# Shorter TensorE bursts, later uses of transposed data and a fourth weight buffer in a two-layer hybrid decoder trunk

## The chip, the cores and the metric

The kernel runs on one core of one Trainium2 chip. The metric is device time in microseconds (us) of one launch; lower is better. A core has a matrix engine (TensorE, in the profile PE for products and PEld for weight loads), a vector engine (VectorE, DVE), an activation engine (ScalarE, ACT), GpSimd (POOL) and SyncE (SP), which here only issues DMA transfers. Each engine works through its own queue in order and waits on semaphores for the others. SBUF is the on-chip memory, PSUM the memory into which TensorE writes its products.

## The reference

Two layers over 256 tokens of width 2048, batch 1, all in float32:

```python
for l in range(DEPTH):                                   # DEPTH = 2
    hn = rms_norm(h, norm_w[l])
    proj = hn @ w_in[l]                                  # 2048 x 8208
    dn_qkv, dn_z, dn_b, dn_a, hg_q, hg_f, hg_i, hg_z = split(proj)
    y_a = deltanet_branch(dn_qkv, dn_z, dn_b, dn_a, ...) # 8 heads of 128: conv, SiLU, L2 norm,
                                                         # gated delta rule with a triangular solve
    y_b = hgrn2_branch(hg_q, hg_f, hg_i, hg_z, ...)      # 8 heads of 128: gated linear recurrence
    h = h + concat(y_a, y_b) @ w_out[l]                  # 2048 x 2048
    gate = sigmoid(h @ w_ple_gate[l])                    # 2048 x 2048
    h = h + (p[l] @ w_ple_up[l]) * gate                  # 256 x 2048
return rms_norm(h, final_norm_w)
```

## The kernel before

**Weight steps.** All weights are streamed once from HBM. `make_plan` cuts them into 392 steps, most of them 128 x 1024 numbers (two blocks of 128 rows by 512 columns, 512 KB). For each step SP loads a tile `raw` (`load`), ACT rounds it into `whi`, DVE forms the rest `wlo = raw - whi` (`prep`), and TensorE multiplies (`products`, through line 378): hi by hi, hi by lo and lo by hi, for both halves of the tokens, 12 matmuls of 128 x 512 in a usual step. `ahead(n)` keeps loads four steps and `whi`/`wlo` two steps ahead of TensorE. There are three buffers `raw` (`WRAW = 3`) and three of `whi` and `wlo`.

**Chunks.** A layer is an input stage ("in", 17 chunks), an output stage ("out", 4) and a gate stage ("gate", 4, with "up"). A chunk is up to 512 columns that accumulate in two PSUM banks, one for each half of the tokens, out of three (`pd`). At its end ACT copies the banks out: `evict` (tiles `...et`), `gate_z` (`...zs`) and `hi` (`...iv`). The first step of the next chunk writes its second bank, which is the first bank of the chunk that has just ended, so TensorE waits there for ACT. The name of a tile tells its owner: `dn12kqet` is DeltaNet, layer 1, head pair 2, keys and queries, evicted.

**Mixers beside the weight steps.** Eight mixers per layer (DeltaNet `DN` and HGRN2 `HG`, each for head pairs g = 0 to 3) and one triangular inverse (`Inverse`, tiles `di`) are Python generators. `tick()` runs after each weight step and advances each of them whose delay, counted in steps, is over. The delays are in the tables `DELAY` and `DELAY_AT` (key: kind, pair or layer, step). TensorE's order is kept exactly as it is written; on the other engines a scheduler sets the order from it. The small float32 products of the mixers stand between two weight steps. One such product is two matmul records and two weight loads in the profile, so 64 products are 256 records. The places in question are `pa1` (64 products in one `tick`, HG), `pa16` (32 products, HG) and the stages `pp16`, `px16` (64 each), `pp32`, `px32`, `pp64`, `px64` (32 each) of `Inverse.run`.

**Transposes by DMA.** Several results must be turned by 128 x 128. Some go through TensorE (`turned`, `turn`: four matmuls against the identity into a PSUM bank). Others go by DMA: `apart` lets ACT split the numbers into 16-bit planes and write them to HBM from ACT's queue, `across` reads them back transposed from SP's queue (line 568), and a later step of the generator uses the result. By DMA go k and q of all four DeltaNet pairs (`kq`), f and q of all four HGRN2 pairs (`fq`), v of pairs 0 to 2 (`v` and, after the convolution, `pv`), five of eight results y (`yp`), and three quarters of h between the stages (`g0`, `n1`, `g1`).

Of the kernel before, what the change touches and what calls it, by code (L numbers as in the profile page):

```python
# [8 lines left out]
F32 = mybir.dt.float32  # L9
# [24 lines left out]
def chunk_cols(chunk):  # L34
# [5 lines left out]
DELAY = {  # L40
# [4 lines left out]
}  # L45

DELAY_AT = {
# [14 lines left out]
}  # L62


V_DMA = 0, 1, 2
Y_DMA = 0, 1, 2, 4, 5
# [110 lines left out]
def trunk(ctx: ExitStack, tc: tile.TileContext, head, xT, x, pT, W, par, fw, cst, msk, eye, out):  # L177
# [3 lines left out]
    hp = pool("hres", 1)  # L181
    ap_ = pool("acts", 13)
    wr = pool("wraw", 3)
    ws = pool("wsplit", 3)
# [6 lines left out]
    V, S, G = nc.vector, nc.scalar, nc.gpsimd  # L191
    WRAW = 3

# [182 lines left out]
    class PEOrder:  # L376
        def matmul(self, *a, **k):
            return tc.keep_in_program_order(nc.tensor.matmul(*a, **k))  # L378

# [3 lines left out]
    PE = PEOrder()  # L383
    live = []

    def spawn(gen):
        live.append([gen, 0])
        advance(live[-1])
# [24 lines left out]
    LOOK, LOAD = 2, 4  # L413
    state = dict(next=0, loaded=0, prepped=0, squared=0)

# [58 lines left out]
    def run_step(psums, act):  # L474

        n = state["next"]
        s = steps[n]
        ahead(n)
        for parts in (range(3),) if s["first"] or s["last"] else ((0, 1), (2,)):
            for m in range(2):  # L480
                products(n, m, psums, act, parts=parts)
        del ready[n]
        state["next"] = n + 1
        if s["what"] != "up":
            tick()
        return s
# [64 lines left out]
    def apart(src, name, into=None):  # L551

        n, c = src.shape[1:]
        for t in range(n):
            yield 1
            if not t:
                flat = (tmp if n * c == 512 else et_tile)(name + "pl") if into is None else into
                flat = u16(flat).rearrange("p (n w c) -> p n w c", n=n, w=2)
            S.copy(flat[:, t], u16(src[:, t]).rearrange("p (c w) -> p w c", w=2))
        d = dr.tile([256 * n * c], U16, tag=f"tr{n * c}", name=name + "d", bufs=4)  # L560
        nc.scalar.dma_start(out=d.rearrange("(n p x) -> p n x", n=n, p=128), in_=flat.rearrange("p n w c -> p n (w c)"))
        return d, c, n * c
# [131 lines left out]
    class Inverse:  # L694
# [24 lines left out]
        def run(self):  # L719
# [38 lines left out]
            pp = bank("pp16")  # L758
            for i in range(NT):
                for b in blocks:  # L760
                    PE.matmul(pp[b:b + 32, 16 * i:16 * i + 16], Bt[b:b + 32, i, b:b + 32], Tn[b:b + 32, i, 0:16],
                              start=True, stop=True)
# [4 lines left out]
            px = bank("px16")  # L767
            for i in range(NT):
                for b in blocks:
                    PE.matmul(px[b:b + 32, 16 * i:16 * i + 16], Pp[b:b + 32, 32 * i:32 * i + 32],  # L770
                              Tt[b:b + 32, i, b + 16:b + 32], start=True, stop=True)
# [5 lines left out]
            for b in (0, 64):  # L777
                V.transpose(Tn[b:b + 32], Tt[b:b + 32, :, b:b + 32])
            yield self.wait("t32")
            pp = bank("pp32")  # L780
            for i in range(NT):
# [4 lines left out]
            for b in (0, 64):  # L786
                S.copy(Pp[b + 32:b + 64], pp[b + 32:b + 64])
            yield self.wait("p32")
            px = bank("px32")
            for i in range(NT):  # L790
# [9 lines left out]
            for T, sl in zip(Tn, parts):  # L800
# [3 lines left out]
                V.transpose(T[32:64, :, 0:32], Tt[0:32, sl, 32:64])  # L804
            yield self.wait("t64")
            pp = [bank(f"pp64{j}") for j in range(len(parts))]
            for i in range(NT):
# [5 lines left out]
            for P_, p in zip(Pp, pp):  # L813
                S.copy(P_[64:128], p[64:128])
            yield self.wait("p64")
            px = [bank(f"px64{j}") for j in range(len(parts))]
            for i in range(NT):
# [8 lines left out]
    class DN:  # L826
# [145 lines left out]
        def dv(self, ps, c0):  # L972
            n, kq, g = self.n, self.kq, self.g
            et, e = evict(ps, c0, 256, self.row.rt, n + "v")
            if g in V_DMA:
                x = yield from apart(et, n + "v", e[:, 512:1024])
                yield self.wait("ve")
                t = across(x, n + "v")
                yield self.wait("vc")
            else:  # L980
                yield self.wait("vp")
                t = turned(et, 0, n + "pvc")
# [3 lines left out]
            V.tensor_tensor(ac, ac, sg, ALU.mult)  # L986
            if g in V_DMA:
                x = yield from apart(ac.unsqueeze(1), n + "pv")
# [63 lines left out]
    class HG:  # L1052
# [19 lines left out]
        def hfhq(self, ps, c0):  # L1072
            x = yield from apart(evict(ps, c0, 512, self.row.rt, self.n + "fq")[0], self.n + "fq")
            yield self.wait("e")
            t = across(x, self.n + "fq")
            yield self.wait("c")
            spawn(self.f_side(t[:, 0:512]))
            spawn(self.q_side(t[:, 512:1024]))

# [17 lines left out]
        def q_side(self, qr):  # L1097
# [76 lines left out]
            xs += factors((8,))  # L1174
            yield self.wait("a")

            A = hA
            Ad = mix("hAd", 128, 1, n + "Ad").rearrange("p (i c) -> p i c", i=4)
            pa = bank("1")
            for i in range(4):  # L1180
                for b in range(0, 128, 32):
                    PE.matmul(pa[b:b + 32, 48 * i:48 * i + 48], k4[:, i, b:b + 32], q8[:, 4 * i + b // 32, :],
                              start=True, stop=True)
            products(UNITS[1:4], xs, pa, 192)
            w1 = pa[:, :192].rearrange("p (i c) -> p i c", c=48)
# [7 lines left out]
            xs += factors((64,))  # L1193
            yield self.wait("u16")
            pb = bank("16")
            products(UNITS[4:], xs, pb, 384)
# [342 lines left out]
```

## Time and profile before

| What | us |
|---|---|
| median of 3 runs (1246.39 to 1248.14) | 1247.51 |
| the profiled execution, its own time | 1244.3 |
| its span, from first to last instruction | 1242.6 |
| TensorE busy, share of the span | 1203.8 (97%) |
| VectorE busy | 877.7 (71%) |
| ScalarE busy | 829.5 (67%) |
| DMA, mean rate | 206 GB/s |

The span is the profiled execution from its first to its last instruction; the 1.7 us beside it lie outside. "Busy" on TensorE counts a matmul from its start to its modelled end, and matmuls overlap: 97% busy does not mean that no time is lost, because slow and stretched matmuls count as well. A view of waits names for each idle stretch the instruction that came next and what released it; "issue" there means that the profile shows nothing that the engine waited for. The granted clock (PEclk) is the share of its full clock that TensorE was given.

### The profile page before, as it was taken

What the parts mean: (1) busy time and instruction counts of PE and PEld (TensorE: products, weight loads), DVE (VectorE), ACT (ScalarE), POOL (GpSimd) and SP (SyncE); (2) the same over time, 40 slices, a digit from 0 to 9 for tenths busy, and PEclk for the clock granted to TensorE, in tenths of its full rate; (3) what the DMA queues carried; (4) which work ended last, traced back from release to release, by engine and by line L of the source; (5) the groups of instructions that cost most, each with busy time, mean ns of one, the idle gap of its engine ahead of it and who ended that gap; (6) DMA issues with size and microseconds to landing.
All of it is one profiled execution on the core that took longest, in us unless ns stands there. A gap on an engine that the chain in (4) does not pass through costs nothing.

```text
span 1242.6 us, 21219 instructions
## 1 busy us (share of the span) xinstructions
PE 1203.8 (97%) x8066; PEld 1002.4 (81%) x8066; DVE 877.7 (71%) x1537; ACT 829.5 (67%) x1418; POOL 81.7 (7%) x67
## 2 busy tenths in 40 slices
PE   9999999997999999999999999999999999999997
PEld 8877788886887888888888788878787878888886
DVE  7677787886756866546667677977786778565565
ACT  7677777676767766547667677677677776664453
POOL 0300010000100010000003000102000000000021
PEclk9999999998999999999999999999999999999999
DMA  8666756576568557756866677666756576687663
GB/s 287 224 205 212 225 193 208 178 238 179 163 203 233 170 162 230 251 189 200 255 221 220 191 229 238 195 180 206 214 146 202 188 220 183 213 256 222 185 203 136
DMA packets 159974, 256.43 MB, mean 206 GB/s; under 512 B 91520, under 2 KB 98560, under 8 KB 159872
## 3 DMA queue, kind: packets, MB, share of 16 engines
q1 hardware_dynamic: 138912, 230.81, 60.2%
q10 hardware_dynamic: 20960, 24.27, 6.0%
q8 instruction: 63, 1.03, 0.3%
q14 instruction: 39, 0.32, 0.1%
HBM read 212.84 MB, written 23.33 MB: 190 GB/s over the span
## 4 chain that ended last, share of the span: by engine, by line
PE 74%; DMA 8%; DVE 7%; ACT 6%; issue 3%; SPq 1%; ACTq 0%; POOLq 0%; POOL 0%; DVEq 0%
PE out L378 14%; PE gate L378 13%; PE in1hi L378 6%; PE in1dk L378 5%; PE in0hi L378 5%; PE in0dv L378 5%; PE in1hf L378 5%; PE in1dv L378 4%; DMA raw<-W 3%; PE in0dk L378 3%; DVE wlo L441 3%; ACT whi L439 3%; PE in0hf L378 2%; PE up L378 2%; SPq L568 1%
## 5 line engine op out<-in xcount | busy, mean ns | idle before, releaser
L441 DVE TENSOR_TENSOR wlo<-raw,whi 128x1024 fp32r<-128x1024 f32 (+2 forms) x393 | 481.0, 1228 | 273.1 <-ACT whi L439 271.0
L439 ACT ACTIVATE whi<-raw 128x1024 fp32r<-128x1024 f32 (+2 forms) x393 | 409.1, 1045 | 238.9 <-DMA raw<-W 55.5
L378 PE MATMUL in1hi<-whi,n1hi 128*128 128x512 f32 x128 | 41.2, 403 | 2.2 <-ACT dn13zs L665 1.8
L378 PE MATMUL in1hf<-whi,n1hi 128*128 128x512 f32 x128 | 41.1, 402 | 1.5 <-ACT hg11zs L665 1.5
L378 PE MATMUL in1dk<-whi,n1hi 128*128 128x512 f32 x128 | 40.1, 395 | 2.3 <-ACT dn12kqet L679 2.3
L378 PE MATMUL in1dv<-whi,n1hi 128*128 128x512 f32 (+1 forms) x128 | 36.0, 373 | 4.7 <-ACT hg12zs L665 1.7
L378 PE MATMUL in1hi<-whi,n1lo 128*128 128x512 f32 x128 | 39.6, 391 | 0.0
L378 PE MATMUL in1hf<-whi,n1lo 128*128 128x512 f32 x128 | 39.6, 391 | 0.0
L378 PE MATMUL in1dk<-whi,n1lo 128*128 128x512 f32 x128 | 39.5, 390 | 0.0
L378 PE MATMUL gate<-whi,g0hi 128*128 128x512 f32 x128 | 39.5, 390 | 0.0
L378 PE MATMUL gate<-whi,g0lo 128*128 128x512 f32 x128 | 39.4, 389 | 0.0
L378 PE MATMUL gate<-whi,g1hi 128*128 128x512 f32 (+1 forms) x120 | 35.8, 379 | 0.0
L378 PE MATMUL gate<-whi,g1lo 128*128 128x512 f32 (+1 forms) x120 | 35.7, 379 | 0.0
L378 PE MATMUL in1dk<-wlo,n1hi 128*128 128x512 f32 x128 | 35.7, 390 | 0.0
L378 PE MATMUL in1hi<-wlo,n1hi 128*128 128x512 f32 x128 | 35.6, 390 | 0.0
L378 PE MATMUL in1hf<-wlo,n1hi 128*128 128x512 f32 x128 | 35.6, 389 | 0.0
L378 PE MATMUL gate<-wlo,g0hi 128*128 128x512 f32 x128 | 35.5, 389 | 0.0
L378 PE MATMUL in1dv<-whi,n1lo 128*128 128x512 f32 (+1 forms) x128 | 34.8, 364 | 0.0
L378 PE MATMUL gate<-wlo,g1hi 128*128 128x512 f32 (+1 forms) x120 | 32.4, 379 | 0.0
L378 PE MATMUL in1dv<-wlo,n1hi 128*128 128x512 f32 (+1 forms) x128 | 31.6, 364 | 0.1
L378 PE MATMUL in0hi<-whi,n0hi 128*128 128x512 f32 x96 | 31.6, 412 | 0.0
L378 PE MATMUL in0hf<-whi,n0hi 128*128 128x512 f32 x96 | 30.9, 403 | 0.1
(1394 smaller groups left out, 2908.7 us busy)
## 6 DMA issues: line engine op xcount, KB each, us to landing
raw<-W SPq DMA_DIRECT2D x383, 512.0 KB, 4.0
raw<-W SPq DMA_DIRECT2D x7, 544.0 KB, 4.1
h<-x SPq DMA_DIRECT2D x4, 512.0 KB, 6.1
xt<-xT SPq DMA_DIRECT2D x3, 512.0 KB, 6.6
out_dram<-h SPq DMA_DIRECT2D x5, 256.0 KB, 2.3
di0d<-di0Bt ACTq DMA_DIRECT2D x4, 256.0 KB, 2.3
di1d<-di1Bt ACTq DMA_DIRECT2D x4, 256.0 KB, 2.3
fw<-fw ACTq DMA_DIRECT2D x2, 512.0 KB, 7.3
```

The costliest lines, as they stand in the source:

```text
L378: return tc.keep_in_program_order(nc.tensor.matmul(*a, **k))
L439: S.activation(hi[:, sl], raw[:, sl], AF.Copy)
L441: V.tensor_tensor(lo[:, sl], raw[:, sl], hi[:, sl].bitcast(F32), ALU.subtract)
L568: nc.sync.dma_start_transpose(u16(t).rearrange("p (k r) -> p k r", k=c // 128), d.rearrange("(r c) -> r c", c=c))
```

## The change

It has five parts.

1. *Bursts.* `PEOrder.matmul` counts the float32 products since the start of the weight step (`state["small"]`). A generator that comes to a burst now yields `calm`, which holds it until fewer than 32 were issued in this step. `pa1`, `pp16` and `px16` are cut in two halves of 32 products, with a weight step between them.
2. *Delays.* The steps behind a DMA transpose are put later (keys `c`, `e`, `ve`, `vc`, `vt`, `vq`, `ye`, `yt`, `t`: from 2 or 3 to 4, and single entries), and many single delays are other numbers.
3. *Planes.* `apart` writes each half to HBM by a DMA of its own as soon as its plane is there. The planes of 512 columns lie in two tiles of the pool `tmp` (six buffers) in place of one of the pool `et` (two buffers).
4. *Buffers.* Four `raw` buffers in place of three; the pool of activations (`acts`) has 12 in place of 13.
5. *Transposes.* f and q of pair 3 and v (before and after the convolution) of pair 2 go through TensorE: 16 more 128 x 128 transposes in each layer, and three DMA transposes fewer.

```diff
 DELAY = {
-    "d": {'c': 3, 'D': 4, ..., 'e': 2, 've': 2, 'vc': 3, 'vp': 1, 'vt': 2, 'vq': 3, 'ye': 2, 'yt': 3, ...},
+    "d": {'c': 4, 'D': 4, ..., 'e': 4, 've': 4, 'vc': 4, 'vp': 1, 'vt': 4, 'vq': 4, 'ye': 4, 'yt': 4, ...},
...
-V_DMA = 0, 1, 2
+FQ_DMA = 0, 1, 2
+VC_DMA = 0, 1
+PV_DMA = 0, 1
...
-    ap_ = pool("acts", 13)
-    wr = pool("wraw", 3)
+    ap_ = pool("acts", 12)
+    wr = pool("wraw", 4)
...
         def matmul(self, *a, **k):
+            state["small"] += a[2].dtype == F32
             return tc.keep_in_program_order(nc.tensor.matmul(*a, **k))
...
+    calm = lambda: state["small"] < 32
...
     def apart(src, name, into=None):
         n, c = src.shape[1:]
+        d = dr.tile([256 * n * c], U16, tag=f"tr{n * c}", name=name + "d", bufs=4)
+        rows = d.rearrange("(n p x) -> n p x", n=n, p=128)
+        if c == 512:
+            into = [None] * n
+        else:
+            into = [into[:, c * t:c * t + c] for t in range(n)]
         for t in range(n):
             yield 1
-            if not t:
-                flat = (tmp if n * c == 512 else et_tile)(name + "pl") if into is None else into
-                flat = u16(flat).rearrange("p (n w c) -> p n w c", n=n, w=2)
-            S.copy(flat[:, t], u16(src[:, t]).rearrange("p (c w) -> p w c", w=2))
-        d = dr.tile([256 * n * c], U16, tag=f"tr{n * c}", name=name + "d", bufs=4)
-        nc.scalar.dma_start(out=d.rearrange("(n p x) -> p n x", n=n, p=128), in_=flat.rearrange("p n w c -> p n (w c)"))
+            flat = u16(tmp(f"{name}pl{t}") if into[t] is None else into[t])
+            S.copy(flat.rearrange("p (w c) -> p w c", w=2), u16(src[:, t]).rearrange("p (c w) -> p w c", w=2))
+            nc.scalar.dma_start(out=rows[t], in_=flat)
         return d, c, n * c
...
             pp = bank("pp16")
             for i in range(NT):
+                if i in (0, NT // 2):
+                    if i:
+                        yield 1
+                    yield calm
...
-            products(UNITS[1:4], xs, pa, 192)
+            products(UNITS[1:2], xs[:1], pa, 192)
+            yield self.wait("a2")
+            yield calm
+            products(UNITS[2:4], xs[1:], pa, 256)
```

Line numbers move: TensorE's line 378 becomes 381, the rounding into `whi` (439) becomes 443, the DMA transposes (568) become 576. Counted over the program, 126 weight steps in place of 113 have small products or transposes behind them, and the largest such group has 38 operations where it had 96.

**First place: TensorE, layer 0, chunk hi2.** `di0pp` is a stage of the inverse, `hg02pa` the products of HGRN2 pair 2, `in0hi` the weight steps. Before:

```order
L378 MATMUL in0hi_1_3103<-wlo_3213,n0hi_231 128x512 x2
L378 MATMUL di0pp_3307<-di0T_3192,di0Bt 32x32 x32
L378 MATMUL hg02pa_3346<-hg02q,hg02k 32x48 x16
L378 MATMUL hg02pa_3346<-hg02X_3084 32x16 x16
L378 MATMUL hg02pa_3346<-hg02X_3203 32x16 x16
L378 MATMUL hg02pa_3346<-hg02X_3258 32x16 x16
L378 MATMUL in0hi_0_3102<-whi_3269,n0hi_316 128x512 x2
```

In the changed kernel:

```order
L381 MATMUL in0hi_1_3080<-wlo_3345,n0hi_404 128x512 x2
L381 MATMUL hg02pa_3462<-hg02q,hg02k 32x48 x16
L381 MATMUL hg02pa_3462<-hg02X_3250 32x16 x16
L381 MATMUL in0hi_0_3079<-whi_3379,n0hi_410 128x512 x2
L381 MATMUL in0hi_0_3079<-whi_3379,n0lo_411 128x512 x2
L381 MATMUL in0hi_0_3079<-wlo_3380,n0hi_410 128x512 x2
L381 MATMUL in0hi_1_3080<-whi_3379,n0hi_410 128x512 x2
L381 MATMUL in0hi_1_3080<-whi_3379,n0lo_411 128x512 x2
L381 MATMUL in0hi_1_3080<-wlo_3380,n0hi_410 128x512 x2
L381 MATMUL hg02pa_3462<-hg02X_3335 32x16 x16
L381 MATMUL hg02pa_3462<-hg02X_3369 32x16 x16
```

Where 96 products (384 records) stood in one row, 32 and 32 now stand with a weight step between them; the stage of the inverse is in an earlier step.

**Second place: ACT, layer 1, the end of the chunk with k and q of pair 2.** `dn12kqet` is the eviction of its first bank, `whi` the rounding of weights, `dn11sg` and `dn10sg` steps of a sigmoid of another pair. Before:

```order
L439 ACTIVATE whi_7049<-raw_7004 128x1024
L500 ACTIVATE dn11sg_7296<-dn11qac 128x512
L507 ACTIVATE dn11sg_7253<-dn11sg_7253 128x512
L508 ACTIVATE dn11sg_7253<-dn11sg_7253 128x512
L679 ACTIVATE dn12kqet<-in1dk_0_6889,s1rt 128x512
```

In the changed kernel:

```order
L512 ACTIVATE dn10sg_7073<-dn10sg_7073 128x512
L513 ACTIVATE dn10sg_7073<-dn10sg_7073 128x512
L443 ACTIVATE whi_7057<-raw_7010 128x1024
L443 ACTIVATE whi_7078<-raw_7031 128x1024
L687 ACTIVATE dn12kqet<-in1dk_0_6896,s1rt 128x512
```

Three sigmoid steps stood between the last rounding and the eviction; now the eviction follows two roundings at once.

**Third place: ACT, layer 0, the result y of HGRN2 pair 0.** `hg00ypd` is the write of its plane to HBM, `hg00hi` the first use of what comes back transposed as `hg00yptr`. Before:

```order
L561 DMA hg00ypd<-hg00yppl 128x1024
L439 ACTIVATE whi_2502<-raw_2454 128x1024
L439 ACTIVATE whi_2521<-raw_2479 128x1024
L679 ACTIVATE hg02fqet<-in0hf_0_2334,s0rt 128x512
L528 ACTIVATE hg00hi_2612<-hg00yptr,pr 128x512
```

In the changed kernel:

```order
L569 DMA hg00ypd<-hg00yppl_2731 128x1024
L443 ACTIVATE whi_2797<-raw_2713 128x1024
L443 ACTIVATE whi_2852<-raw_2743 128x1024
L505 ACTIVATE hg02qsg<-hg02fqtr 128x512
L1157 ACTIVATE hg01X_2990<-hg01X_2990 128x512
L512 ACTIVATE hg02fsg<-hg02fsg 128x512
L513 ACTIVATE hg02fsg<-hg02fsg 128x512
L512 ACTIVATE hg02qsg<-hg02qsg 128x512
L443 ACTIVATE whi_2885<-raw_2795 128x1024
L513 ACTIVATE hg02qsg<-hg02qsg 128x512
L1157 ACTIVATE hg01X_3060<-hg01X_3060 128x512
L533 ACTIVATE hg00hi_3239<-hg00yptr,pr 128x512
```

Two roundings and one eviction stood between the write and the use; now three roundings and seven other operations do. Over the whole program, 14 of 47 DMA transposes were used within two weight steps of their write (counted in roundings on the engine that uses them); now 3 of 41 are.

More of the change, by code (lines that the diff above doesn't have):

```diff
@@ L191, in trunk @@
     V, S, G = nc.vector, nc.scalar, nc.gpsimd
-    WRAW = 3
+    WRAW = 4
     h = [hp.tile([128, 2, 512], F32, name=f"h{c}") for c in range(4)]
@@ L413, in trunk @@
     LOOK, LOAD = 2, 4
-    state = dict(next=0, loaded=0, prepped=0, squared=0)
+    state = dict(small=0, next=0, loaded=0, prepped=0, squared=0)
     def load(n):
@@ L477, in run_step @@
         s = steps[n]
+        state["small"] = 0
         ahead(n)
@@ L768, in run @@
             for i in range(NT):
+                if i in (0, NT // 2):
+                    if i:
+                        yield 1
+                    yield calm
                 for b in blocks:
@@ L779, in run @@
             yield self.wait("t32")
+            yield calm
             pp = bank("pp32")
@@ L788, in run @@
             yield self.wait("p32")
+            yield calm
             px = bank("px32")
@@ L805, in run @@
             yield self.wait("t64")
+            yield calm
             pp = [bank(f"pp64{j}") for j in range(len(parts))]
@@ L815, in run @@
             yield self.wait("p64")
+            yield calm
             px = [bank(f"px64{j}") for j in range(len(parts))]
@@ L974, in dv @@
             et, e = evict(ps, c0, 256, self.row.rt, n + "v")
-            if g in V_DMA:
+            if g in VC_DMA:
                 x = yield from apart(et, n + "v", e[:, 512:1024])
@@ L986, in dv @@
             V.tensor_tensor(ac, ac, sg, ALU.mult)
-            if g in V_DMA:
+            if g in PV_DMA:
                 x = yield from apart(ac.unsqueeze(1), n + "pv")
@@ L1072, in hfhq @@
         def hfhq(self, ps, c0):
[L1073 to L1078, printed above, removed]
+            et, _ = evict(ps, c0, 512, self.row.rt, self.n + "fq")
+            if self.g in FQ_DMA:
+                x = yield from apart(et, self.n + "fq")
+                yield self.wait("e")
+                t = across(x, self.n + "fq")
+                yield self.wait("c")
+                spawn(self.f_side(t[:, 0:512]))
+                spawn(self.q_side(t[:, 512:1024]))
+            else:
+                yield self.wait("p")
+                spawn(self.f_side(turned(et, 0, self.n + "pf")))
+                spawn(self.q_side(turned(et, 256, self.n + "pq")))
         def f_side(self, fs):
@@ L1175, in q_side @@
             yield self.wait("a")
+            yield calm
             A = hA
@@ L1183, in q_side @@
                               start=True, stop=True)
-            products(UNITS[1:4], xs, pa, 192)
+            products(UNITS[1:2], xs[:1], pa, 192)
+            yield self.wait("a2")
+            yield calm
+            products(UNITS[2:4], xs[1:], pa, 256)
             w1 = pa[:, :192].rearrange("p (i c) -> p i c", c=48)
@@ L1194, in q_side @@
             yield self.wait("u16")
+            yield calm
             pb = bank("16")
```

34 rows, old and new, of tables (DELAY, DELAY_AT) are left out of this document.

## The prediction

> **What bounds the kernel now.** I read the page's busy times first, then one row of the chain of waits, TensorE's waits, the timeline at the longest of them, and the clock around them.
>
> ```profile
> span 1242.6 us, 21219 instructions
> PE 1203.8 (97%) x8066; PEld 1002.4 (81%) x8066; DVE 877.7 (71%) x1537; ACT 829.5 (67%) x1418; POOL 81.7 (7%) x67
> 470.68 57.15 PE out L378 x252
> q8 instruction: 63, 1.03, 0.3%
> ```
>
> TensorE is the bound: busy for 97% of the span. The chain's row shows a stretch without disturbance: 252 matmuls of 128 x 512 in 57.15 us, 227 ns each, so a usual weight step of 12 costs 2.72 us. The change touches none of these matmuls; it can gain only where TensorE stands or is slowed. The last row is the fetch of TensorE's own instructions: 1.03 MB in 63 packets. TensorE has 8066 + 8066 = 16132 records, so a packet carries 256 of them (64 bytes each).
>
> The view of TensorE's waits says where it stands:
>
> ```profile
> PE hg02pa L378 <- issue: 5.1, 1, 5.1
> PE in0hi L378 <- ACT dn03zs L665: 3.0, 1, 3.0
> ...
> PE in1dk L378 <- ACT dn12kqet L679: 2.3, 1, 2.3
> PE in0hf L378 <- ACT dn03kqet L679: 1.8, 1, 1.8
> PE in1hi L378 <- ACT dn13zs L665: 1.8, 1, 1.8
> PE in1dv L378 <- ACT hg12zs L665: 1.7, 1, 1.7
> PE in1dv L378 <- ACT dn10vet L679: 1.6, 1, 1.6
> PE in1hf L378 <- ACT hg11zs L665: 1.5, 1, 1.5
> PE in0hi L378 <- ACT hg00fqet L679: 1.3, 1, 1.3
> PE in0dv L378 <- ACT whi L439: 1.2, 2, 1.0
> PE in0dk L378 <- ACT dn02kqet L679: 0.8, 1, 0.8
> PE dn00po L378 <- DVE dn00v L1032: 0.7, 1, 0.7
> PE in1dv L378 <- issue: 0.7, 1, 0.7
> ```
>
> There are two families. "issue" stands in bursts of small products, where nothing that the profile shows was missing. The rows with ACT are weight steps that write into a PSUM bank which ACT has not emptied yet. Everything else is small: even the longest row here for the rounded weights (`whi`) is 1.2.
>
> **The change, part by part.** All sums are made against the profiled execution, 1244.3 (span 1242.6 and 1.7 around it), which is 3.2 below the median of 1247.51.
>
> *1. Bursts: what they cost.* The timeline of TensorE at the two long "issue" waits, and the windows behind them (columns: length, busy us of PE, PEld, DVE, ACT, POOL, granted clock, DMA share, GB/s):
>
> ```profile
> 276.70 1.26 PE L378 MATMUL di0pp<-di0T,di0Bt 32*32 32x16 f32 x128
> 277.89 1.03 PE L378 MATMUL hg01pa<-hg01X 128*32 128x16 f32 x60
> 281.89 0.31 PE L378 MATMUL hg01pa<-hg01X 128*32 128x64 f32 x4 [2.97 <-issue]
> ...
> 299.48 1.00 PE L378 MATMUL hg02pa<-hg02X 128*32 128x16 f32 x90
> 305.61 0.30 PE L378 MATMUL hg02pa<-hg02X 128*32 128x16 f32 x6 [5.13 <-issue]
> ```
> ```profile
> 281.90:286.50 4.60, 4.60 (x16) 3.16 (x16) 3.90 (x12) 3.92 (x10) 0.00 (x0) 0.66 0.66 234
> 299.10:305.60 6.50, 1.38 (x128) 1.26 (x122) 1.66 (x3) 1.68 (x3) 0.00 (x0) 0.87 0.96 321
> 305.60:310.90 5.30, 5.29 (x18) 4.20 (x19) 2.03 (x9) 1.24 (x2) 0.00 (x0) 0.52 0.77 124
> 405.40:409.00 3.60, 3.54 (x13) 3.12 (x14) 2.94 (x10) 2.78 (x6) 0.00 (x0) 0.62 0.23 93
> ```
>
> At the first place TensorE stops after 128 + 60 of 192 matmuls. At the second the order ahead shows 96 products, 192 matmuls, and 6 were left. With as many loads that is over 370 records in a row, and then it stands for 3 to 5 us in the middle of products whose operands were there. More than one fetch packet's 256 records had gone by in some 2.2 us, and in the longer stall the DMA engines were busy to 0.96. I read this as TensorE out of instructions, its next packet queued behind other transfers. Behind both stalls the granted clock is low: 0.66 over 4.60 us and 0.52 over 5.30 us, which loses (1 - 0.66) x 4.60 = 1.6 and (1 - 0.52) x 5.30 = 2.5. With at most 38 operations in a group and a weight step of 2.72 us between, a packet of 256 records lasts for more than one group. So the gaps (5.1 + 3.0 + 0.7 = 8.8) and the lost clock (4.1) go: 12.9. Bounds: 0, if the stalls only move, to -12.9. I take **-12.5**, near the upper end, because no group in the changed kernel comes near the 384 records of both long stalls.
>
> *2. What cutting costs.* There are 13 more weight steps with small work behind them. What an interruption costs beyond its products:
>
> ```profile
> 187.35 0.55 PE L378 MATMUL hg00pa<-hg00q,hg00k 128*32 128x48 f32 x32
> ...
> 188.67 0.73 PE L378 MATMUL in0hf<-whi,n0hi 128*128 128x512 f32 x2
> 189.24 0.62 PE L378 MATMUL in0hf<-whi,n0lo 128*128 128x512 f32 x2
> 189.71 0.62 PE L378 MATMUL in0hf<-wlo,n0hi 128*128 128x512 f32 x2
> ...
> 208.09 0.39 PE L378 MATMUL in0hi<-wlo,n0hi 128*128 128x512 f32 x1
> 208.41 1.14 PE L378 MATMUL hg00pa<-hg00X 128*32 128x16 f32 x64
> 209.48 0.73 PE L378 MATMUL in0hi<-whi,n0hi 128*128 128x512 f32 x2
> ```
>
> Behind the small work two matmuls take 0.57 (188.67 to 189.24) where the next two take 0.47: 0.10. Ahead of it the last large matmul takes 0.32 (208.09 to 208.41) where 0.23 is usual: 0.09. That is 0.19 an interruption, 2.5 in all. By another reading, 64 products in one take 1.32 (187.35 to 188.67) and 32 take 1.07 (208.41 to 209.48), so two halves would cost 2 x 1.07 - 1.32 = 0.82 more, or 10.7 in all. The two rows differ in shape and in what they follow, so I take the edges: **+2.5**, bounds 0 (the edges are already in other steps) and +10.7.
>
> *3. Evictions on ACT.* The change writes the order of the steps anew, and what stands on ACT at the ends of chunks is other work. Before, the eviction of the second place waited behind a sigmoid:
>
> ```profile
> 708.34 0.63 ACT L500 ACTIVATE dn11sg<-dn11qac 128x512 f32<-128x512 f32 x1 [2.14 <-DVE dn11qac L879]
> ...
> 710.06 0.67 ACT L679 ACTIVATE dn12kqet<-in1dk,s1rt 128x512 f32<-128x512 f32 x1
> ```
>
> ACT itself waited 2.14 us for DVE there; the eviction queued behind it, and TensorE behind the eviction: its 2.3. In the changed order six such evictions stand right behind a rounding: 2.3 + 1.8 + 1.6 + 1.5 + 1.3 + 0.8 = 9.3, of which I count 9. The three gate evictions `zs` (3.0 + 1.8 + 1.7, and the low clock of 0.62 behind the first, (1 - 0.62) x 3.60 = 1.4: 7.9) keep other work ahead of them; I count half, 4. In turn some evictions get work of the new pair-3 path ahead of them; by the small ACT rows above (0.8 to 1.8) I charge 1.5. Together **-11.5**; bounds 0, if other work slips in everywhere, and with all of them gone and nothing new, -(9.3 + 7.9) = -17.2.
>
> *4. Transposes back on TensorE.* 16 more of 128 x 128 in each layer, in eight groups of four:
>
> ```profile
> 466.87 0.60 PE L381 MATMUL dn03yp<-cs,dn03yt 128*128 128x128 f32 x4
> 467.22 0.71 PE L378 MATMUL out<-whi,hg02hi 128*128 128x512 f32 x2
> ```
>
> Four cost 0.35 (466.87 to 467.22), so 8 x 0.35 = 2.8; I take **+3.0**, with an edge of 0.19 for one group that stands alone. Bounds: 2.8 and, with an edge at each of the eight, 4.3.
>
> *5. Delays behind DMA transposes.* The longest waits of ACT that end on such a transfer:
>
> ```profile
> ACT dn02kac L875 <- DMA dn02kqtr<-dn02kqd: 6.1, 1, 6.1
> ...
> ACT whi L439 <- DMA raw<-W: 55.5, 47, 5.4
> ```
>
> Two steps later is 2 x 2.72 = 5.4 us more for the transfer, so most of these waits go. On TensorE that is worth nothing by itself: what is queued on ACT behind them is the rounding, which runs two steps ahead, and the waits for `whi` on TensorE are 1.2 at most. On SP, where the transposed read waits for the write and the weight loads queue behind it, a later read waits less. I count **0**: the cover is the two steps of 2.72 us each; if it were gone, the 6.1 us row shows the size of one miss, 6.1 - 5.4 = 0.7.
>
> *6. Planes, buffers, activations.* ACT issues 21 more DMA writes, and has fewer plane copies (66 to 60 of 1024 columns, 12 to 8 of 512).
>
> ```profile
> 866.37 0.40 ACTq L561 DMA_DIRECT2D hg12fqd<-hg12fqpl  x1
> ```
>
> 21 x 0.40 = 8.4 us more in ACT's queue. ACT is busy 67% of the span, so this lies in its idle time; the fourth `raw` lets a load start a step earlier, so the 55.5 us that ACT waits for weights shrink, but nearly all of that is cover, not path. POOL's queue has 82 us of work and is passed by nothing here. With one buffer fewer for activations no wait for one shows before that could grow. **0**, bounds -1.2 (the longest `whi` row) and +1.7 (one such miss like the 1.7 of `hg12zs`, an ACT operation that came late).
>
> The sum: -12.5 + 2.5 - 11.5 + 3.0 + 0 + 0 = -18.5, so 1244.3 - 18.5 = 1225.8 for a profiled execution, and 1229.0 as a median.
>
> **The rivals.**
>
> *The bursts were not starved.* The stalls then stay, moved to other places. Against it: both long stalls come at the end of 384 records, and the burst of 128 matmuls at 187.35 passes without one. For it: in layer 1 a burst of 192 matmuls passes too, so the length alone does not set the stall. The time is 1229.0 + 12.5 = 1241.5. [...]
>
> *The evictions stay late.* ACT's other work at the ends of chunks changes places with the old: 1229.0 + 11.5 = 1240.5. For it: ACT waits 2.14 us for DVE in the row shown, and such a row can stand ahead of any eviction. Against it: six named places are followed by the rounding alone in the new order.
>
> *All of the evictions come in time*, with nothing new: 17.2 in place of 11.5, and the waits of 1.2 for `whi` and 0.7 of `dn00po` gone as well: 5.7 + 1.2 + 0.7 = 7.6, so 1221.4. For it: in the changed order most ends of chunks have the rounding right ahead. Against it: the three `zs` evictions, the longest of these rows, keep other work ahead of them.
>
> *Slower: the DeltaNet chain is squeezed.* Its state runs TensorE, DVE or ACT, TensorE four times for each pair and layer, 32 hand-overs, one weight step apart. Before, one of them shows, the 0.7 of `dn00po`. Now pairs 1 and 2 run on consecutive steps, beside f and q of HGRN2's last pair on the same ACT and DVE. If each hand-over came late by more than (18.5 + 2.5) / 32 = 0.66 us, close to the wait shown, the kernel would be slower than before by over 2.5, beyond 1250. Against it: DVE and ACT are idle 29% and 33% of the time, and 31 of 32 hand-overs fit now.
>
> **How the numbers follow.** The forecast gets 0.65, its own range 1223 to 1237 by the bounds of the evictions below and the cutting cost above; evictions all in time 0.13; bursts not starved 0.07; evictions late 0.08; DeltaNet squeezed 0.07. The forecast is the likeliest: 1229.0. The range of 1217 to 1242 takes in the two cases near 1241 and the one at 1221, with 2.5 of cutting cost that may not come and some of its own error, and leaves out the slower one, the case where two of the others come together, and the tail of the cutting cost. A difference under 0.2%, 2.5 us, is about what a measurement of this kernel can tell from none. The cases at 1221 and 1229 are faster beyond it; those at 1241 as well, though with the cutting cost at its upper bound they give the 0.05 for no change. Faster 0.88, same 0.05, slower 0.07.
>
> **What would show it.** Right: TensorE's waits without "issue" rows over 1 us in `hg01pa` and `hg02pa`; no window with a granted clock near 0.5 behind a burst; the rows of `dn12kqet`, `dn03kqet`, `dn10vet`, `hg11zs`, `hg00fqet` and `dn02kqet` gone, of `zs` some left; four more transposes costing 0.35 each time; `whi` rows on TensorE still near 2 in all. Wrong: "issue" rows of the old size in other small products, rows of `po`, `pw` or `pz` with DVE or ACT as releaser, or edges of 0.4 and more around each of the 13 new interruptions, with the stretched matmuls outside of any wait.

## The result and the profile after

The changed kernel takes **1214.62 us** (median of 6 runs, 1213.62 to 1215.79), beside 1246.95 for the kernel before on the same chips (1241.1 to 1253.23): a ratio of 0.974, with a 95% interval of 0.9711 to 0.9769. The forecast was 1229.0, with a range of 1217 to 1242. The sign and the places were right; the gain is 32 us where 18.5 were forecast, and the time lies 2.4 us below the range.

The page after, its busy times, fetch row and clock:

```profile
span 1212.1 us, 21290 instructions
PE 1200.7 (99%) x8098; PEld 1001.7 (83%) x8098; DVE 876.6 (72%) x1537; ACT 823.1 (68%) x1408; POOL 77.1 (6%) x67
q8 instruction: 63, 1.03, 0.3%
core 0: 1212.1 us, clock 0.999
```

TensorE's waits, all of them (line 381 is the old 378, 384 the old 381):

```profile
PE gate L381 <- ACT whi L443: 1.3, 1, 1.3
PE warm L381 <- DVE zeros L256: 1.1, 1, 1.1
PE in0dz L381 <- ACT n0ahi L281: 0.4, 1, 0.4
PE hg13yp L384 <- DVE hg13yt L655: 0.3, 1, 0.3
PE hg03yp L384 <- DVE hg03yt L655: 0.3, 1, 0.3
```

Both families of the forecast are gone: not one "issue" row, and not one eviction. The view's rows add up to 30.2 us before and 3.4 after, so 26.8 us come from waits. Before, TensorE also worked at half its clock in three stretches, behind the two long "issue" waits and behind the wait on `dn03zs`:

```profile
283.37:286.78 3.41, 3.41 (x28) 2.25 (x30) 2.91 (x9) 3.36 (x9) 0.00 (x0) 0.50 0.51 198
305.61:310.68 5.07, 5.07 (x17) 4.00 (x18) 2.03 (x9) 1.02 (x2) 0.00 (x0) 0.50 0.79 127
406.25:409.66 3.41, 3.41 (x13) 3.02 (x12) 2.79 (x8) 2.36 (x5) 0.00 (x0) 0.50 0.06 24
```

There large matmuls start 0.43 us apart, beyond the stretches 0.23. By the granted clock half of each stretch is lost, an estimate of 1.7 + 2.5 + 1.7 = 5.9 us. In the changed kernel the clock is 1.00 up to the last matmul, which ends at 1204.2. The waits cost somewhat more than their rows say: a row begins at the modelled end of the matmul before, 0.39 us after its start, while the next large matmul usually starts after 0.23. Summed over the waits ahead of large matmuls, that is 2.8 us before and 0.5 now, 2.3 less. On the other side stand the costs: the small work between two large matmuls, beyond the usual 0.23 and without waits, takes 105.5 us in 118 places before and 110.4 in 131 places now, 4.9 more. In all 26.8 + 5.9 + 2.3 - 4.9 = 30.1, beside the 30.5 by which the spans differ.

One more row moved, on another engine: ACT's wait for raw weights, 55.5 us in 47 waits before:

```profile
ACT whi L443 <- DMA raw<-W: 7.6, 10, 1.9
```

### The profile page after: what moved, and what is told of

It reads as the page before. It is cut to its first block, busy times and chain, and to the rows that moved or that the text cites. A ratio compares the mean times of both kernels' runs of the same rounds, so it can differ in the third digit from the quotient of the medians.

```text
span 1212.1 us, 21290 instructions
## 1 busy us (share of the span) xinstructions
PE 1200.7 (99%) x8098; PEld 1001.7 (83%) x8098; DVE 876.6 (72%) x1537; ACT 823.1 (68%) x1408; POOL 77.1 (6%) x67
## 4 chain that ended last, share of the span: by engine, by line
PE 95%; ACT 2%; DMA 1%; DVE 1%; issue 1%; POOLq 0%; POOL 0%; ACTq 0%; DVEq 0%
PE out L381 14%; PE gate L381 11%; PE in1hi L381 7%; PE in0hi L381 7%; PE in0hf L381 7%; PE in0dk L381 7%; PE in1hf L381 7%; PE in1dk L381 7%; PE in0dv L381 7%; PE in1dv L381 7%; PE up L381 1%; PE in0dz L381 1%; DMA raw<-W 1%; PE in1dz L381 1%; ACT whi L443 0%
```

## The experiments

The runs take the change apart: one part alone on the kernel before, or one part undone in the changed kernel. Ratios are to the kernel before on the same chip.

**1. Is it the length of a burst, or where it falls?** I counted TensorE's records (matmuls, weight loads and its 60 sequencer records) against the starts of the 63 fetch packets in the trace of before. Of the packets k = 0 to 62, 43 start when 150 to 200 records beyond 256 x k have begun, the earliest at 153. In both long stalls the packet started only at 449, 0.7 and 2.7 us after TensorE had stopped there, and TensorE went on some 2.3 us after that start. Taking 165 as the usual place, 449 - 165 = 284 records seem to be in hand when a packet is asked for; if they run out before it is usable, TensorE stands. This is a reading of the count, and the runs test it. Experiment e1 moves every burst by 128 records against the blocks and cuts nothing:

```
         warm(6)
+        zz = zeros.bitcast(F32)
+        for _ in range(32):          # e2: 16
+            PE.matmul(warm_ps[0:32, 0:16], zz[:, 0:32], zz[:, 0:16], start=True, stop=True)
```

> The kernel before with 32 small dummy products (128 TensorE records) ahead of the first weight step, where TensorE waits for the first weights anyway; nothing is cut or moved. Phase theory: the profile of before shows each fetch packet starting some 165 records into a block of 256, and a stall when about 284 more records ran before it could be used; the three stalls are the three places where 284 records from such a point take the least time (1.7, 1.7 and 3.1 us). Moved by 128 records the shortest such stretch takes 3.8 us: the issue waits of 9.0 us fall under 1, the low-clock windows behind them go, and the time falls by 12.9 less 0.6 for the dummies, to a ratio near 0.990. Length theory (384 records in a row run dry wherever they stand) and load theory (the packet is late because the DMA engines are full at that place): issue waits stay near 9 us, ratio 1.000 to 1.001.

> The same with 16 dummy products (64 records). Phase theory: the two long stalls stay at their places (284 records in 1.4 and 1.9 us), the third, of 0.7, goes, and a small one may come in the first burst of HGRN2 pair 1 (3.3 us): issue waits 7 to 10 us in all. If any disturbance of the start removed the stalls, this kernel would lose them too.

e1 took 1241.62 beside 1250.4: ratio 0.9924 (0.9898 to 0.995). The timeline of TensorE at the first stalled burst, and the window over the place of the second:

```profile
279.18 1.26 PE L381 MATMUL di0pp<-di0T,di0Bt 32*32 32x16 f32 x128
280.37 1.14 PE L381 MATMUL hg01pa<-hg01X 128*32 128x16 f32 x64
281.44 0.74 PE L381 MATMUL in0hi<-whi,n0ahi 128*128 128x512 f32 x2
300.00:312.00 12.00, 12.00 (x112) 9.62 (x110) 6.85 (x18) 4.21 (x6) 0.00 (x0) 1.00 0.95 256
```

The same 384 records run through in 2.26 us (279.18 to 281.44) where 5.43 were needed before (276.70 to 282.13). Over the place of the second, the clock is full although the DMA engines are 0.95 busy. The issue waits fell from 9.0 to 0.3 us, in one row:

```profile
PE in1hi L381 <- issue: 0.3, 1, 0.3
```

In e2 (one run, 1250.12) they stay at their places:

```profile
PE hg02pa L381 <- issue: 4.2, 1, 4.2
PE hg01pa L381 <- issue: 3.6, 1, 3.6
PE dn00po L381 <- DVE dn00v L1035: 3.0, 1, 3.0
```

So the stall depends on where a burst falls against the blocks, not on its length alone, and not on a full DMA alone. The gain of e1, 9.5 us by the ratio, is less than the 12.9 forecast, because evictions come up in place of stalls:

```profile
PE in0dv L381 <- ACT hg02zs L668: 4.7, 1, 4.7
PE in1dv L381 <- ACT whi L442: 2.8, 2, 2.0
PE in0hf L381 <- ACT hg01zs L668: 2.5, 1, 2.5
```

None of these three was over 1.2 before. The likely reason, which no run tests by itself, is that ACT caught up while TensorE stood without instructions.

**2. Whole bursts in the changed kernel.** e4 issues `pa1`, `pp16` and `px16` whole again, in the second of their two steps, and replaces the condition behind `calm` with `True`. e10 keeps `calm`. e11 is e4 with the 32 dummy products. Only the first loop is shown; `px16` and `pa1` are alike.

```
             pp = bank("pp16")
+            yield calm
+            yield 1
             for i in range(NT):
-                if i in (0, NT // 2):
-                    if i:
-                        yield 1
-                    yield calm
```

> The changed kernel with its bursts whole again: all 64 products of pa1, pp16 and px16 are issued in the second of their two steps, and nothing holds a burst back when another stands in the same step; all else stays. Phase theory: one stretch of 284 records takes 1.5 us (di0px with the burst of HGRN2 pair 1), all others over 4.4: one issue wait of 2 to 4 us with 1 to 2 us of low clock behind it, ratio to before near 0.977. Length theory: a stall at every burst of 256 records and more, over 10 us, ratio 0.985 or more. If cutting costs what I charged (2.5 us), the uncut bursts give that back; if it costs nothing, they don't.

> The changed kernel as it is, on one chip with the next two, so that differences of a few us can be told: ratio to before 0.972 to 0.976 by both theories, no issue waits.

> The changed kernel with pa1, pp16 and px16 whole (64 products, 256 records, in the second of their two steps), but still held back where another burst stands in the same step. Phase theory: the shortest stretch of 284 records takes 4.0 us, so there is no issue wait over 0.5, though the bursts are as long as two of the three that stalled in part before; and 12 interruptions fewer give back what cutting costs. By the run with whole bursts and one stall that is about 0.3 us each: 3 to 4 us faster than the changed kernel, ratio 0.970 to 0.972. Length theory: bursts of 256 records stall again, slower than the changed kernel.

> The changed kernel with whole bursts, nothing held back, and 32 dummy products at the start. Without the dummies this kernel had one issue wait of 3.4 us (384 records in a row) and a low clock behind it; moved by 128 records the shortest stretch takes 4.1 us. Phase theory: no issue wait over 0.5, 4 to 5 us faster than without the dummies, 2 to 4 us faster than the changed kernel: ratio 0.970 to 0.973. Length theory: the stall stays, ratio 0.974 or more.

e4: 1217.65, ratio 0.9737 (0.9718 to 0.9755), the same as the changed kernel. It has one stall, at the place that the count named (384 records in a row), with the low clock of 0.58 behind it at a DMA share of 0.02:

```profile
PE hg01pa L381 <- issue: 3.4, 1, 3.4
277.80:282.60 4.80, 4.80 (x15) 3.80 (x14) 3.49 (x10) 0.97 (x2) 0.00 (x0) 0.58 0.02 5
```

The other three ran on one chip. The changed kernel itself (e9): 1217.71 (1216.34 to 1219.71); in this profile TensorE waits 5.9 us, where 3.4 stand above, and 0.6 of it is for an eviction. e10: **1213.15** (1212.59 to 1216.1), ratio 0.9708 (0.9672 to 0.9744). e11: **1213.18** (1210.3 to 1215.98), ratio 0.9705 (0.9668 to 0.9742). The runs of both lie below all six of the changed kernel. The largest issue wait is 0.4 in e10:

```profile
PE hg01pa L381 <- issue: 0.4, 1, 0.4
```

and 0.6 in e11, at another burst, a little over what was expected. So cutting the bursts was not needed once their place was right, and it costs: e10 has 10 interruptions of the weight steps fewer, and saves 4.6 us by the medians and 2.2 by the spans of the two profiled executions (1216.6 and 1214.4): 0.2 to 0.5 us each. Between the large matmuls of the same two traces the small work takes 2.4 us less, 0.24 each. Both versions beat the changed kernel, by 0.4%.

**3. The fourth buffer.** e5 is the changed kernel with `WRAW = 3`, `pool("wraw", 3)` and `pool("acts", 13)`; e6 the kernel before with 4, 4 and 12.

> The changed kernel with three raw buffers and 13 of activations again; all else stays. Buffer theory: between the two profiles ACT's waits of the rounding for raw weights fell from 57 to 9 us, and what is queued on ACT behind a late rounding is late too, the evictions among it. So the fourth buffer carries most of what my forecast missed: with three, ACT waits 40 us and more for raw, TensorE waits 8 to 15 us again on evictions and roundings, ratio to before 0.982 to 0.988. My prediction's theory (the buffer is worth nothing on TensorE's path, the order of the steps is all): the same as the changed kernel within 1.5 us, ratio near 0.974. Issue waits stay at 0 in both.

> The kernel before with four raw buffers and 12 of activations, nothing else. Buffer theory: ACT's waits for raw fall from 57 us to 10 to 20, TensorE's waits on evictions from 16.8 to 8 or less, the issue waits stay (the order of records is the same): ratio 0.990 to 0.994. Prediction's theory: no change within 1.5 us, ratio 0.999 to 1.001. If the DMA queue is the limit, not the number of buffers (SP waits for a transposed write with loads behind it), the waits for raw stay near 50 us and the ratio near 1.

e5: 1222.66 beside 1244.75, ratio 0.9827 (0.9809 to 0.9845). e6: 1233.48, ratio 0.9907 (0.9886 to 0.9928). ACT's wait for raw weights in e5, then in e6:

```profile
ACT whi L443 <- DMA raw<-W: 83.2, 62, 6.8
```
```profile
ACT whi L439 <- DMA raw<-W: 6.8, 4, 3.5
```

The buffer takes these waits from 55.5 to 6.8 by itself, and is worth 0.9% either way: 0.9827 - 0.974 = 0.0087, 10.8 us, when it is undone, 11.6 when it is done alone. In e5 TensorE's waits come to 9.1 us, 5.7 more than in the first profile of the changed kernel and 3.2 more than in e9. They are not evictions, which come to 0.7 in all, but 5.1 on the split weights themselves, most of it in the gate stage. The longest row of each kind:

```profile
PE gate L381 <- ACT whi L443: 3.8, 2, 2.6
PE in0hf L381 <- ACT dn02zs L673: 0.4, 1, 0.4
```

Half clock for 3.41 us behind the longest of these waits costs another 1.7 us. On evictions and roundings together that is less than the 8 to 15 us that the buffer theory expected. In e6 waits on evictions stay at 13.3 us, above the 8 expected.

**4. The planes.** e8 is the changed kernel with the old `apart`; e14 the kernel before with the new one.

```
-            S.copy(flat.rearrange(...), ...)
-            nc.scalar.dma_start(out=rows[t], in_=flat)
+            S.copy(flat[:, t], ...)
+        nc.scalar.dma_start(out=..., in_=flat...)      # one write for both planes
```

> The changed kernel with the two planes of each DMA transpose written by one DMA from one tile as before. Prediction's theory: 0, ratio near 0.974 (within 1.5 us of the changed kernel). Rival: with the delays of 4 steps the later, single write is late for the transposed read, so that SP waits longer for it with weight loads behind it, and ACT's waits for raw rise from 9 to 20 us and more, with 3 to 6 us on TensorE: ratio 0.977 to 0.979.

> The kernel before with the two plane writes alone. Undone in the changed kernel they cost 0.9%. If they are worth that by themselves, ratio 0.989 to 0.993 and ACT's waits on DMA transposes fall from 48 to 35 us or less. If with three buffers ACT stands for raw weights anyway (57 us), little of it reaches TensorE: ratio 0.996 to 1.001.

e8: 1223.29, ratio 0.983 (0.9812 to 0.9848), 11 us worse than the changed kernel. The rival had the direction but not the way, since raw waits stay at 4.4 us. TensorE waits 9.9 us in e8, 3.4 in the changed kernel. The way to the longest of these waits is in the timelines of e8, in order: the write, the transposed read, then ACT, DVE and TensorE:

```profile
91.96 0.38 ACTq L566 DMA_DIRECT2D dn02kqd<-dn02kqpl  x1
97.57 2.08 SPq L573 DMA_TRANSPOSE dn02kqtr<-dn02kqd  x1
103.37 0.91 ACT L892 ACTIVATE dn02kac<-dn02kqtr,pr 128x256 f32<-128x256 f32 x2 [5.20 <-DMA dn02kqtr<-dn02kqd]
103.91 0.48 DVE L896 SCALAR_TENSOR_TENSOR dn02kac<-dn02kqtr,pr,dn02kac 128x255 f32<-128x255 f32 x1 [4.99 <-ACT dn02kac L892]
110.94 0.45 PE L384 MATMUL dn00ssq<-cs,dn00kq 128*128 128x128 f32 x1 [3.15 <-DVE dn00QK L977]
```

One write of 512 KB holds the read on SP until 97.57. SP's wait for the write of this tile, in e8 and then in the changed kernel:

```profile
SPq L573 <- DMA dn02kqd<-dn02kqpl: 4.9, 1, 4.9
SPq L576 <- DMA dn02kqd<-dn02kqpl: 1.4, 1, 1.4
```

ACT stands for it for 5.2 us, DVE behind ACT for 5.0, the `dn00QK` of *another* pair is queued on DVE behind that, and TensorE waits 3.2 for it. With two writes of 256 KB (the landings of this tile, by the view of DMA issues, are 5.5 us in e8 and 4.0 in the changed kernel) ACT's step starts without a wait:

```profile
95.88 2.48 SPq L576 DMA_TRANSPOSE dn02kqtr<-dn02kqd  x1
101.96 0.49 ACT L895 ACTIVATE dn02kac<-dn02kqtr,pr 128x256 f32<-128x256 f32 x1
```

This step comes only 1.4 us earlier than in e8. That ACT doesn't stand before it is also due to its order there: a rounding and four sigmoid steps fill 98.9 to 102.0, which in e8 stand elsewhere. e8 puts the planes back into the pool of two buffers as well. How much of the 11 us belongs to the write, to the order that the scheduler made of it and to the pool is not shown.

Alone on the old kernel (e14) the planes gain nothing: 1255.14, ratio 1.0038 (1.0012 to 1.0064), with ACT's waits for raw weights at 96.9 us and those on transposes at 43 where they were 48. Both expectations missed; with three buffers the second write made it a little slower.

**5. Delays.**

> The kernel before with the changed kernel's tables of delays alone: bursts whole, three raw buffers, planes and transposes as before. If the delays alone bring the evictions in time, TensorE's waits on ACT evictions fall from 16.8 us to under 3, with the clock behind them, about 18 us; the bursts land at other phases, where the record count shows one short stretch (2.1 us, di1px), so issue waits near 1 to 2 us in place of 9.0: ratio 0.975 to 0.980. If my prediction's halved share for the gate evictions was right, waits on ACT stay at 5 to 8 us, ratio near 0.983. If the evictions need the fourth buffer, they stay near 16 us, ratio 0.990.

> The kernel before with the new delays and four raw buffers (12 of activations); bursts, planes and transposes as before. With three buffers the delays gave nothing (1.0006): ACT waited 85 us for raw, and TensorE for late DeltaNet keys (3.6 and 3.3 us) and for pair 3's results at the output stage (2.7, 2.7, 1.4, 1.4). If the buffer is what the delays lacked, raw waits fall under 20 us and the ratio is 0.982 or less. If the single plane write and pair 3 by DMA hold it, the waits on the DeltaNet keys and at the output stage stay, and the ratio is 0.988 to 0.994, no better than the buffer alone.

e3, the new tables alone: 1251.08, ratio 1.0006 (0.9984 to 1.0028), which no theory had. Other waits come in place of the old ones:

```profile
PE dn10ssq L381 <- DVE dn10QK L960: 3.6, 1, 3.6
PE dn00ssq L381 <- DVE dn00QK L960: 3.3, 1, 3.3
PE in1hf L378 <- ACT hg10zs L665: 3.0, 1, 3.0
PE dn13yp L381 <- DVE dn13yt L647: 2.7, 1, 2.7
PE dn03yp L381 <- DVE dn03yt L647: 2.7, 1, 2.7
```

The first two are the late DeltaNet keys of e8, the last two results of pair 3 that come late into the output stage. e12, with four buffers as well: 1239.33, ratio 0.9914 (0.9886 to 0.9942), no better than the buffer alone; the waits for raw weights fall from 83.4 to 4.0 us, those on the keys (3.8 and 1.9) and on pair 3 (2.7 and 2.7) stay. But only one row of an eviction is left:

```profile
PE in0dk L378 <- ACT dn02kqet L679: 1.4, 1, 1.4
```

Four profiles now part the delays from the buffer. TensorE's waits on evictions are 16.8 us in the kernel before, 13.3 with the buffer alone (e6), 9.8 with the delays alone (e3) and 1.4 with both (e12).

**6. The transposes.** e7 sets `FQ_DMA = 0, 1, 2, 3` and `VC_DMA` and `PV_DMA` to `0, 1, 2` in the changed kernel.

> The changed kernel with f and q of HGRN2 pair 3 and v of DeltaNet pair 2 through DMA again: 32 transposes off TensorE, three DMA transposes more in each layer. Cost theory of my prediction: 2.8 to 4.3 us less on TensorE, and nothing lost: ratio 0.971. Latency theory: by the order, the products of HGRN2 pair 3 then come some 9 weight steps later (26 us), behind the end of the input stage; its y comes into the output stage late, and TensorE waits for it and for the late DeltaNet steps, 5 to 15 us: ratio 0.978 to 0.985.

e7: 1238.56, ratio 0.9952 (0.9933 to 0.9971), beyond even the latency theory. 0.9952 - 0.974 = 0.021, 26 us:

```profile
PE dn13yp L384 <- DVE dn13yt L655: 4.0, 1, 4.0
PE hg13yp L384 <- DVE hg13yt L655: 3.5, 1, 3.5
PE hg03yp L384 <- DVE hg03yt L655: 3.5, 1, 3.5
PE dn03yp L384 <- DVE dn03yt L655: 2.7, 1, 2.7
```

All of TensorE's waits are 17 us more than in the changed kernel, and the clock is at half for 3.41 and again for 6.83 us around these waits in each layer, up to 10 us more.

**7. Buffer, planes and shifted bursts together, without delays and transposes.**

> The kernel before (its delays, whole bursts, DMA transposes) with four raw buffers, the two plane writes and the 32 dummy products that move the fetch. If buffer, planes and phase carry the gain by themselves, TensorE's waits on evictions fall under 5 us and the ratio is 0.975 to 0.980. If the order of the evictions is a term of its own, as the prediction had it (11.5 us), the waits on zs and kqet evictions stay at 10 us and more, as with the buffer alone (13 us), the issue waits go, and the ratio is 0.981 to 0.987.

e13: 1241.98, ratio 0.9933 (0.991 to 0.9957), outside both expectations. Over its runs it is no better than the shift alone. ACT's waits for raw weights are 22.4 us and the stalls of before are gone (two issue rows of 1.3 and 0.8 stand at other places), but TensorE waits 19 us on evictions, more than before:

```profile
PE in0dv L381 <- ACT hg02fqet L685: 5.5, 1, 5.5
PE in0dv L381 <- ACT hg02zs L671: 3.9, 1, 3.9
PE in1hi L381 <- ACT dn13zs L671: 3.8, 1, 3.8
PE in0hi L381 <- ACT dn03zs L671: 2.3, 1, 2.3
```

So the order of the steps was a term of its own, as the forecast had it, and the gains do not add. Alone, the shift is worth 9.5 us, the buffer 11.6, delays nothing, planes less than nothing; undone, the buffer costs 11, the planes 11, the transposes 26, and the cuts nothing or less.

## Why the prediction was off, point by point

The forecast's terms of gain were -12.5 (bursts) and -11.5 (evictions), 24.0 in all; the two profiles show 26.8 of waits, 5.9 of clock and 2.3 hidden in the rows, 35.0. Its costs were 5.5, and the profiles show 4.9. The two differences, 11.0 and 0.6, make up nearly all of the 12.0 us between -18.5 and -30.5.

- *Bursts, -12.5.* Right in size: 9.0 us of issue waits went, and 4.2 of low clock behind them, 13.2 in all. The mechanism, a packet that comes too late, stands (in both long stalls it started at record 449, 0.7 and 2.7 us after TensorE had stopped); that it queued behind other transfers is not shown, and its trigger was wrong. "No group comes near 384 records" is not what counts: e1 passes 384 records in 2.26 us. By the count of part 1 the records since the packet was asked for matter, and the changed kernel takes 5.4 us at least for 284 of them from such a point, where the stalled places took 1.6, 1.6 and 3.1.
- *Cutting, +2.5.* Within its bounds of 0 and 10.7: e10 against e9 gives 0.2 to 0.5 for each interruption where 0.19 was taken. What the forecast did not ask is whether the cuts were needed.
- *Evictions, -11.5.* The term that fell short: of the 11.0 us of gain that were missed, about 9 are here. All of the 16.8 us in waits on evictions went, with 1.7 of clock and most of the 2.3 hidden in the rows; the forecast counted half of the `zs` rows, left out 1.0 us of small rows and charged 1.5 for new waits that did not come. It had the order of the steps as the one thing that moves these waits. The order was needed but did not do it alone: with the new delays and three buffers (e3) 9.8 us of evictions stand, `zs` rows of 3.0 and 2.6 among them; with buffer and planes and the old order (e13) 19 us do; with the new delays and the buffer (e12) 1.4.
- *Buffers and planes, 0, with bounds of -1.2 and +1.7.* This is the step that failed, and with it the term above came out too small. "Nearly all of that is cover, not path" was said of the 55.5 us that ACT waits for weights. Undone in the changed kernel the buffer costs 10.8 us and the planes 11. The low bound was taken from the waits for `whi` on TensorE, 1.2 at most. With the changed kernel's order and three buffers (e5) TensorE waits 5.1 us for the split weights themselves, 1.7 of clock follow, and evictions show 0.7; with the delays on the kernel before (e3 and e12) the same buffer takes 8.4 us of waits on evictions away. So what the late weights hold up depends on what stands behind them on ACT, and it can show in TensorE's view under the name of an eviction. In e5 more waits and the clock together make up 5 to 7 of the 10.8 us; where the rest goes is not shown. The 6.1 us that ACT waited for `dn02kac` before are of the same kind: in part 4 such a wait reaches TensorE as 3.2 us on the keys of another pair.
- *Transposes, +3.0.* As a cost it is nearly right: each group of four stands beside other small work and adds 0.44 us to it where 0.35 was taken, 3.5 in all. As a term it missed what they buy: pair 3 in time for the output stage, with the new delays 26 us.
- *Delays, 0.* Right alone (1.0006), wrong as a part: only with the buffer, the planes and the transposes do they leave hardly a wait.
- *The rivals.* Bursts not starved: refuted. Evictions late: refuted in the changed kernel, and just what e13 does. All evictions in time, 1221.4: what happened. It counted 26.5 of waits and 5.5 of clock, close to the 26.8 and 5.9 of the profiles; what it missed is mainly what the rows of waits hide. It was given a chance of 0.13, because the three `zs` rows keep other work ahead of them in the new order; that work is short, though: ahead of `dn03zs` ACT idles for 0.75 us, then does one eviction and one step of 0.6 us, where before it came to the same place without a pause behind steps of two sigmoids. The DeltaNet chain squeezed: rows of `po`, `pw` or `pz` are absent after; in e2 one such hand-over shows 3.0.

What stays open: no run takes the new delays out of the changed kernel alone, so their part in it rests on e3, e12 and e13. The prices of the parts when undone add up to more than the 32 us, so they are not shares of it.

## What to carry to other kernels

A wait on an engine beside the path is not free because the engine has idle time: here ACT was busy for 67% of the span, and the buffer that took 48.7 us of its waits for weights away was worth 11.6 us (e6). Ask what is queued behind such a wait, and look for the same lateness on the bounding engine under another name. Price a part that only gives slack (a buffer, an earlier write, a delay) by the waits that it can take away together with the others, not alone; here such parts were worth from less than nothing to 12 us alone, and 11 us (the buffer, the planes) to 26 us (the transposes) when undone in the finished kernel. For bursts of small matmuls count the records between two fetch points: here moving the bursts by 128 records took the issue waits from 9.0 to 0.3 us (e1), and the kernel with cut bursts has none.

## What the runs showed that was not expected

By the reading of the count in part 1 (165 records as the usual start of a packet, 449 in both long stalls) TensorE seems to have had only about 284 records in hand when it asked for the next 256. Places that ran them in 1.8 us or less stood for 3.0 to 5.1 us in every run that had one (before, e2, e4, e6, e14). Places at 2.9 to 3.2 us stood for anything from nothing (e2, e14) to 2.6 us (e12), and from 4.0 us on at most 0.8 showed (e13). So the place of a burst alone doesn't set the stall, which suggests that the time until the packet comes varies too.

Around the three longest waits of the kernel before (2.97, 5.13 and 3.00 us) the granted clock was 0.50 for 3.41, 6.83 (303.85 to 310.68, from inside the wait) and 3.41 us, also with the DMA engines nearly idle (0.06 in the third of the three stretches), and in e1 it was 1.00 with them 0.95 busy: in these traces it went with the standstill and not with the traffic. The length of a wait alone doesn't decide it: 1.85 us for the eviction `dn12kqet` were followed by half the clock in e6, and 2.3 us for the same eviction left it full in the kernel before. The 3.41 us behind this eviction, before and in e6:

```profile
710.78:714.19 3.41, 3.41 (x15) 2.81 (x16) 1.73 (x3) 3.41 (x8) 0.00 (x0) 1.00 0.49 168
```
```profile
705.81:709.22 3.41, 3.41 (x9) 2.63 (x9) 1.56 (x2) 3.41 (x8) 0.00 (x0) 0.50 0.53 166
```

The kernel before spread over 15 us from run to run on one chip (1243.67 to 1258.96), the changed one over 3.4.
